# Two-layer backbone on one core: pooling mixer emitted one group later, products reordered, operand regions shifted, first and last classical tiles changed

## The chip, the cores and the metric

The program runs on one core of a Trainium2 chip. A core has a matrix engine (PE, whose weight loads the profile lists apart as PEld), a vector engine (DVE), a scalar engine (ACT), a general engine (POOL) and a queue processor (SP). Each works through its own instruction list in order and waits on semaphores for the others. The metric is the device time of one launch, in microseconds (us). Data is staged in on-chip SBUF; matmuls write PSUM.

## The reference, cut to what matters

```python
for i in range(2):                                   # layer 0: mLSTM mixer, layer 1: pooling mixer
    sh1, sc1, g1, sh2, sc2, g2 = split(silu(c) @ ada_w[i] + ada_b[i], 6)
    xn = rmsnorm(x, norm1_g[i]) * (1 + sc1) + sh1
    if i == 0:
        y = mlstm_mixer(xn, cn, ...)                 # projections, chunkwise scan in two directions, output product
    else:                                            # rows of 64 tokens, 4 groups of 256 channels
        p = centred_mean(xn, window of the group: 2, 4, 8 or 16) - xn
        y = einsum(p, pool_w[group]) * pool_scale
    x = x + g1 * y
    u = rmsnorm(x, norm2_g[i]) * (1 + sc2) + sh2
    x = x + g2 * (square(relu(u @ w1[i])) @ w2[i])   # 1024 -> 4096 -> 1024
return rmsnorm(x, final_g)                           # x: 1024 tokens x 1024 channels, float32
```

## The kernel before

All work is in float32. A big product is made of three matmuls on split operands (`mm3`, L169): weight-high by input-high, weight-high by input-low, weight-low by input-high. `split` (L165) makes the high part on ACT (L166) and the low part on DVE (`sub`, L163). The activations x lie feature-major in SBUF as tiles of [128, 2, 512]: four tiles for each of the two token halves (hf = 0 and 1).

A scheduler orders each engine's list: it simulates the program, and where several instructions are ready the code that was emitted first goes first. So the place of a `yield` in a generator, and the windows in which generators are woven together, decide the order.

One MLP goes in these stages.

1. `up_halves`: a few blocks of 128 hidden channels ("classical": 6 in layer 0, 12 in layer 1) are computed for one token half at a time by `up_half` (L858), eight k blocks of three matmuls into one PSUM bank. The inputs are uh (high, made by DVE L818 and ACT L819) and ul (low, DVE L820); the weights w1h and w1l come from ACT and DVE.
2. `flow`: the other hidden channels go through a scheme with seven products for eight, and their results hs are stored to DRAM on POOL's queue (L950).
3. Still in `flow`: 16 early classical steps of the second product (two for each of eight output blocks m; PSUM tile pd), then the passes: products (PSUM tile pe) whose operands hop are read back by `load_op` (L1005) on POOL's queue into two rings of buffers, A (12) and T (16), as the table RING says. A third ring B (4) holds raw hidden channels.
4. The classical tiles of the second product: first all output blocks of half 0, then those of half 1. Their operands hc are split from hr, which SP reads back. A step is one output block by one chunk of the hidden channels. The result goes into x by DVE (L1180).

`beside` runs side generators in windows of the main one's steps: `mods1` (layer 1's adaLN vectors: 48 loads of 256 KB on POOL's queue and a DVE product each, L237 and L238) in the window MO; the pooling mixer `pool(0)` and the norm of half 0 for layer 1's MLP in the windows ML, beside the classical tiles of layer 0; `pool(1)` and the norm of half 1 beside `up_halves(1, 0)` in the window MU.

A norm's statistics are: the squares of x (ACT L298) summed over the tiles into acc (L300, on DVE or POOL), a small matmul pc over partitions (L273), rv (DVE L275), a power on POOL (L276), dgr (DVE L279), a matmul rbp that spreads the result (L281), and a copy rbs (ACT L284). From rbs the next u is made (L818, L819, L820). `pool(hf)` makes for each of four groups a padded copy up (L1258), sums s over shifted copies (L1263, L1267), corrections at the row edges (POOL, L1275), the difference pt (L1276), and then, at once, the matmul pp (L1284) and the update of x (L1286).

Two places are called turns below: turn 1, from the end of layer 0's classical tiles to the first blocks of layer 1 (half 0), and turn 2, from half 0 to half 1 of those blocks.

In the address of a partition, tiles of ring A begin on a multiple of 256 bytes, those of T 96 bytes past one, those of B 128 bytes past one; weight tiles begin on one. The inputs uh and ul lie in A (for half 1, those of the first two tiles in B), their combinations th and tl, which the seven-product scheme takes, in T. Of the matmuls with 512 columns, 3,300 in the program read their moving operand from A, 504 from B and 2,904 from T.

Of the kernel before, what the change touches and what calls it, by code (L numbers as in the profile page):

```python
# [15 lines left out]
P = 128  # L16
D = 1024
T = 1024
# [44 lines left out]

MO = (49, 16, 86)
ML = ((12, 2, 12), (10, 12, 20))
MU = (34, 0, 10)
# [20 lines left out]
class Net:  # L87
    def __init__(self, ctx, tc, io, dbg=None):
        self.tc = tc
        self.nc = tc.nc  # L90
        self.io = io
        self.ctx = ctx
        e = ctx.enter_context
        self.psA = e(tc.tile_pool(name="psA", bufs=1, space=bass.MemoryType.PSUM))
        self.bank = 0
        self.alt = 0
        self.psN = e(tc.tile_pool(name="psN", bufs=2, space=bass.MemoryType.PSUM))
        self.psC = e(tc.tile_pool(name="psC", bufs=1, space=bass.MemoryType.PSUM))
        self.dr = e(tc.tile_pool(name="dr", bufs=1, space=bass.MemoryType.DRAM))
        self.sb = e(tc.tile_pool(name="sb", bufs=1))  # L100
        self.gx = ExitStack()
        self.gp = self.gx.enter_context(tc.tile_pool(name="gp", bufs=1))
        self.r = None
# [754 lines left out]
    def up_half(self, l, f, hf):  # L858

        nc = self.nc  # L860
        hi, lo = self.load_w(self.io["w1"][l, f], [P, KT, P], "w1")
        ps = self.pa([P, 512], "pu1")
        for k in range(KT):
            self.mm3(ps, hi[:, k], lo[:, k], self.uh[l][k // 2][hf][:, k % 2], self.ul[l][k // 2][hf][:, k % 2], k == 0, k == KT - 1)
        r = self.tmr([P, 512], "r")
        self.hidden(l, f, hf, r, ps)
# [138 lines left out]
    def load_op(self, l, i, q):  # L1005

        t = self.op16("hop", RING[(7 * i + q) % 28])
        self.nc.gpsimd.dma_start(out=t, in_=self.hs[l][i, q])  # L1008
        self.H[i, q] = t
# [9 lines left out]
    def flow(self, l):  # L1019
# [177 lines left out]
        for hf in range(2):  # L1197
            for m in order[:4] if l and hf else order:
                classical(hf, m, ch[hf][::-1] if hf == 0 and m == order[-1] else ch[hf], bank(new), 0, 512, True, result(hf, 0, 512))
        if l:  # L1200
            pn = [bank(lambda: self.pn("pd")) for _ in range(2)]
# [11 lines left out]
        steps[a:b] = self.turns(steps[a:a + 14], steps[a + 14:b])  # L1213
        ready, loads = [], 0
        for n, (_, _, run, what) in enumerate(steps):
            halves = n > b
# [11 lines left out]
            elif what == "C" and self.late:  # L1228
                self.late.pop(0)()
            pump()  # L1230
            yield


    def pool(self, hf):
# [7 lines left out]
        if hf:  # L1242
            yield from self.rstd(hf, g)
        rb = self.rb
        for a in range(4):
# [4 lines left out]
            pt = [tmp([P, 512], "pt") for _ in range(2)]  # L1250
            for i in range(2):
                k = 2 * a + i

                u = tmp([P, 8, 80], "up")
                g.memset(u[:, :, 0:8], 0.0)
# [3 lines left out]
                                       in1=rb.rearrange("p (r t) -> p r t", r=8), op0=ALU.mult, op1=ALU.mult)  # L1259
                nc.scalar.activation(t, t, AF.Identity, bias=self.mod[1][:, k:k + 1])  # L1260
                lo, hi = 1, 80
                s = tmp([P, 8, 80], "s")
                v.tensor_tensor(out=s[:, :, 1:80], in0=u[:, :, 0:79], in1=u[:, :, 1:80], op=ALU.add)  # L1263
                for b in range(a):
                    w = 1 << b
                    n = tmp([P, 8, 80], "s")
                    v.tensor_tensor(out=n[:, :, lo + w:hi - w], in0=s[:, :, lo:hi - 2 * w], in1=s[:, :, lo + 2 * w:hi], op=ALU.add)  # L1267
# [8 lines left out]
                v.scalar_tensor_tensor(out=pt[i].rearrange("p (r t) -> p r t", r=8), in0=s[:, :, 8:72], scalar=0.5 / w,  # L1276
                                       in1=u[:, :, 8:72], op0=ALU.mult, op1=ALU.subtract)
                yield
            pn = self.pn("pp")
            for i in range(2):  # L1280
                m = 2 * a + i
                ps = pn[:, i]
                for c in range(2):
                    nc.tensor.matmul(out=ps, lhsT=pw[:, c, P * i:P * i + P], rhs=pt[c], start=c == 0, stop=c == 1)  # L1284
                x = self.x[a][hf][:, i]
                v.scalar_tensor_tensor(out=x, in0=ps, scalar=self.pg[:, m:m + 1], in1=x, op0=ALU.mult, op1=ALU.add)  # L1286

            if a == 0:
                self.rs = self.rstd(hf)
            else:  # L1290
                next(self.rs)
            next(self.rs)
            yield

    def final(self, hf, lo, n, last=False):
# [100 lines left out]
    def run(self):  # L1396
        self.weng = None
        self.mark = None
        self.gate = None
        self.nw = 0  # L1400
        self.region("r1")
# [103 lines left out]
```

## Time and profile before

| | |
|---|---|
| median of 3 runs | 2058.02 us (2054.32 to 2061.98) |
| profiled execution, its own time | 2041.83 us |
| span, first to last instruction | 2039.7 us |
| mean granted PE clock, share of full | 0.981 |
| busy: PE / DVE / ACT / POOL | 1932.5 / 1387.6 / 868.7 / 415.2 us |
| chain that ended last, by engine | PE 65%, DMA 10%, DVE 10%, issue 9%, POOL 3%, ACT 2% |

Busy is the time in which an engine worked on an instruction; a wait is the idle time before an instruction, put down to what came last. A line of a kernel can be a helper's, so operations are told by their tiles (pd, pe, pu and ps are PSUM tiles of the products, ws and w1h/w1l weights). [...]

### The profile page before, as it was taken

How to read it: one execution, taken by the hardware profiler on the slowest of the kernel's cores; microseconds unless marked ns; L12 is line 12 of the kernel's file. 1: busy time of each engine (PE TensorE's matmuls, PEld its weight loads, DVE VectorE, ACT ScalarE, POOL GpSimd, SP SyncE). 2: the span in 40 equal slices, each digit the busy share in tenths (PEclk: the TensorE clock that was granted, in tenths of full speed). 3: DMA queues.
4: the chain of work that ended last, by engine and by line, in shares of the span. 5: the costliest groups of instructions: out<-in, count | busy, mean ns of one | idle time of the engine just before them, and what ended most of it. 6: DMA issues, size and time to landing. Idle time of an engine off the chain costs nothing.

```text
span 2039.7 us, 26798 instructions
## 1 busy us (share of the span) xinstructions
PE 1932.5 (95%) x9341; PEld 1544.0 (76%) x9341; DVE 1387.6 (68%) x2492; ACT 868.7 (43%) x1598; POOL 415.2 (20%) x595
## 2 busy tenths in 40 slices
PE   6999999988999999999999999798999998999998
PEld 3998877766777888887777777576888886886787
DVE  5587233878858688864777878587478855568644
ACT  4412222444436566654322233345557654222433
POOL 1222110454420011122332231210011120112010
PEclk9999999999999999999999999798999999999999
DMA  8499567665435366788888462154447696754642
GB/s 308 133 328 328 170 207 222 204 194 172 143 126 171 133 233 222 263 280 307 273 293 270 129 207 95 63 166 141 140 160 240 246 326 224 245 165 161 198 160 89
DMA packets 202167, 414.83 MB, mean 203 GB/s; under 512 B 18864, under 2 KB 108080, under 8 KB 202032
## 3 DMA queue, kind: packets, MB, share of 16 engines
q1 hardware_dynamic: 141936, 227.49, 35.1%
q0 software_dynamic: 43968, 157.31, 22.5%
q10 hardware_dynamic: 16128, 28.32, 3.7%
q8 instruction: 74, 1.21, 0.2%
q14 instruction: 61, 0.50, 0.1%
HBM read 303.31 MB, written 109.74 MB: 203 GB/s over the span
## 4 chain that ended last, share of the span: by engine, by line
PE 65%; DMA 10%; DVE 10%; issue 9%; POOL 3%; ACT 2%; SPq 1%; POOLq 0%; ACTq 0%; DVEq 0%
PE ps L172 22%; PE pd L172 11%; PE pu L172 9%; PE pb L172 6%; PE pe L172 6%; PE po L172 3%; DMA w<-in_w 2%; PE pv L172 1%; POOL adat L237 1%; DMA hr<-hd 1%; DMA qk<-kqd 1%; DMA xr<-xd 1%; PE pp L1284 1%; DVE ws L163 1%; PE pn L748 1%
## 5 line engine op out<-in xcount | busy, mean ns | idle before, releaser
L172 PE MATMUL pe<-hop,ws 128*128 128x512 f32 x1512 | 362.6, 398 | 12.5 <-DVE y L1097 6.2
L172 PEld LDWEIGHTS pe<-hop,ws 128*128 128x128 f32 x1512 | 283.3, 189 | 87.4 <-DVE y L1097 7.7
L172 PE MATMUL pd<-hc,ws 128*128 128x512 f32 (+1 forms) x1440 | 331.3, 386 | 10.4 <-ACT ws L166 4.3
L172 PEld LDWEIGHTS pd<-hc,ws 128*128 128x128 f32 x1440 | 257.5, 189 | 76.4 <-ACT ws L166 7.8
L166 ACT ACTIVATE ws<-w 128x384 fp32r<-128x384 f32 (+3 forms) x296 | 151.8, 529 | 335.8 <-PE pe L172 118.6
L163 DVE TENSOR_TENSOR ws<-w,ws 128x384 fp32r<-128x384 f32 (+3 forms) x296 | 176.0, 605 | 99.1 <-ACT ws L166 98.5
L172 PE MATMUL ps<-th,ws 128*128 128x512 f32 x736 | 242.5, 396 | 0.1
L172 PE MATMUL ps<-uh,ws 128*128 128x512 f32 x552 | 179.4, 391 | 0.0
L172 PEld LDWEIGHTS ps<-th,ws 128*128 128x128 f32 x736 | 138.4, 188 | 33.5 <-issue 0.5
L950 POOL DMA_DIRECT2D hs<-hs x126 | 67.2, 533 | 453.3 <-DVE hs L163 448.9
L172 PE MATMUL ps<-tl,ws 128*128 128x512 f32 x368 | 145.4, 395 | 0.0
L172 PE MATMUL pu<-ul,w1h 128*128 128x512 f32 x288 | 115.7, 402 | 11.2 <-DVE ul L820 11.2
L172 PE MATMUL pu<-uh,w1h 128*128 128x512 f32 x288 | 117.7, 410 | 5.5 <-ACT uh L819 4.6
L172 PEld LDWEIGHTS ps<-uh,ws 128*128 128x128 f32 x552 | 103.6, 188 | 23.4
L163 DVE TENSOR_TENSOR ws<-w1s,ws 128x512 fp32r<-128x512 f32 x138 | 94.7, 687 | 37.7 <-ACT ws L166 37.6
L172 PE MATMUL pu<-uh,w1l 128*128 128x512 f32 x288 | 116.6, 406 | 1.3 <-DVE w1l L163 1.3
L166 ACT ACTIVATE ws<-w1s 128x512 fp32r<-128x512 f32 x138 | 86.6, 629 | 71.7 <-PE ps L172 45.3
L1097 DVE TENSOR_TENSOR y<-pe,y 128x512 f32<-128x512 f32 x128 | 87.5, 686 | 43.1 <-PE pe L172 43.0
L1008 POOL DMA_DIRECT2D hop<-hs x126 | 66.8, 532 | 237.4 <-PE pe L172 143.9
L172 PE MATMUL ps<-ul,ws 128*128 128x512 f32 x276 | 108.1, 392 | 0.0
L935 DVE TENSOR_TENSOR o<-ps,o 128x512 f32<-128x512 f32 x115 | 79.1, 688 | 38.5 <-PE ps L172 35.9
L163 DVE TENSOR_TENSOR hs<-o,hs 128x512 fp32r<-128x512 f32 x126 | 85.8, 686 | 12.7 <-ACT hs L166 12.5
(288 smaller groups left out, 3785.8 us busy)
## 6 DMA issues: line engine op xcount, KB each, us to landing
hs<-hs POOLq DMA_DIRECT2D x126, 512.0 KB, 4.0
hop<-hs POOLq DMA_DIRECT2D x126, 512.0 KB, 5.7
w<-in_w SPq DMA_DIRECT2D x64, 512.0 KB, 4.0
adat<-in_adaT POOLq DMA_DIRECT2D x96, 256.0 KB, 4.8
w1s<-in_w SPq DMA_DIRECT2D x46, 512.0 KB, 5.1
w<-in_w SPq DMA_DIRECT2D x44, 384.0 KB, 3.6
ada<-in_adaT SPq DMA_DIRECT2D x32, 512.0 KB, 5.5
w<-in_w SPq DMA_DIRECT2D x60, 256.0 KB, 3.4
```

What stands on the lines that cost most here:

```text
L163: (eng or self.nc.vector).tensor_tensor(out=lo, in0=src, in1=hi.bitcast(F32), op=ALU.subtract)
L166: self.nc.scalar.activation(hi, src, AF.Copy)
L172: return self.nc.tensor.matmul(out=out, skip_group_check=more, **k)
L237: (nc.gpsimd if l else nc.sync).dma_start(out=w, in_=self.io["adaT"][48 * l + i - 16, :, n * q:n * q + n])
L748: nc.tensor.matmul(out=pn[:, a, d], lhsT=W[d][:, h], rhs=vs[:, h], start=False, stop=d == 1)
L935: self.mark = v.tensor_tensor(out=o[out], in0=o[p], in1=o[q], op=ALU.add)
L950: nc.gpsimd.dma_start(out=self.hs[l][i, q], in_=t)
L1008: self.nc.gpsimd.dma_start(out=t, in_=self.hs[l][i, q])
L1097: self.mark = v.tensor_tensor(out=y, in0=o[bank], in1=y, op=ALU.add)
L1284: nc.tensor.matmul(out=ps, lhsT=pw[:, c, P * i:P * i + P], rhs=pt[c], start=c == 0, stop=c == 1)
```

## The change

The parts of the diff are: other windows MO and ML; a tile of 160 bytes per partition allocated first, which moves the tiles behind it; the order of the 24 matmuls in `up_half`; a POOL copy of one element, that reads the sum evacuated by ACT for an output block, in every other early classical step, after which (and only then) operand loads are issued in these steps; the first two output blocks of half 1 taken in turns by chunk; and `pool`, in which the matmuls of a group come behind the preparation of the next, the edge corrections and half 1's sums acc move from POOL to DVE, pt is one tile and two buffers of s are used in turn.

```diff
-MO = (49, 16, 86)
-ML = ((12, 2, 12), (10, 12, 20))
+MO = (49, 34, 92)
+ML = ((14, 2, 9), (10, 9, 17))
...
+        self.sb.tile([P, 40], F32, name="pad", tag="pad", bufs=1)
...
     def up_half(self, l, f, hf):
...
-        for k in range(KT):
-            self.mm3(ps, hi[:, k], lo[:, k], self.uh[l][k // 2][hf][:, k % 2], self.ul[l][k // 2][hf][:, k % 2], k == 0, k == KT - 1)
+        us = [[u[l][k // 2][hf][:, k % 2] for k in range(KT)] for u in (self.uh, self.ul)]
+        for j, (w, u) in enumerate(((hi, us[0]), (lo, us[0]), (hi, us[1]))):
+            for k in range(KT):
+                self.nc.tensor.matmul(out=ps, lhsT=w[:, k], rhs=u[k], start=j + k == 0, stop=j == 2 and k == KT - 1)
...
     def load_op(self, l, i, q):
...
-        self.nc.gpsimd.dma_start(out=t, in_=self.hs[l][i, q])
+        d = self.nc.gpsimd.dma_start(out=t, in_=self.hs[l][i, q])
+        if self.pace is not None:
+            self.after(d, self.pace)
...
+            if hf:
+                n = 2 * len(ch[1])
+                steps[at:at + 2 * n] = [s for c in range(0, n, 2) for s in steps[at + c:at + c + 2] + steps[at + n + c:at + n + c + 2]]
...
+        n0 = self.pieces(l)[0]
...
-            pump()
+            if n0 <= n < n0 + 16:
+                if (n - n0) % 2:
+                    m = (n - n0) // 2
+                    self.pace = nc.gpsimd.tensor_copy(out=pace, in_=Y[m // 2][0][0:1, m % 2, 0:1])
+                    pump()
+                    self.pace = None
+            else:
+                pump()
...
     def pool(self, hf):
...
-            yield from self.rstd(hf, g)
+            yield from self.rstd(hf)
+        def mix(a, pw, pt):
+            pn = self.pn("pp")
...
-                        g.tensor_tensor(out=e, in0=e, in1=f, op=ALU.mult)
+                        v.tensor_tensor(out=e, in0=e, in1=f, op=ALU.mult)
...
+            if before:
+                mix(*before)
+            before = a, pw, pt
             yield
+        mix(*before)
+        yield
```

With the added tile, A tiles begin 160 bytes past a multiple of 256, B tiles 32 bytes past one, T tiles on one; weight tiles begin 160 bytes past one.

PE's order at turn 1 before: the last matmuls of the pooling mixer (pp), the classical tiles (pd), the statistics (pc, then rbp), and the first two blocks of layer 1 (pu, uh and ul, by w1h and w1l).

```order
L1284 MATMUL pp<-pt,pw 128x512 x2
L172 MATMUL pd<-hc,ws 128x512 x12
L273 MATMUL pc<-cst,acc 128x2 x4
L281 MATMUL rbp<-dgr,cst 128x512
L172 MATMUL pu_11376<-uh,w1h 128x512
L172 MATMUL pu_11425<-uh,w1h 128x512
L172 MATMUL pu_11376<-ul,w1h 128x512
L172 MATMUL pu_11376<-uh,w1l 128x512
L172 MATMUL pu_11376<-uh,w1h 128x512
```

The same place of the changed program:

```order
L1274 MATMUL pp<-pt,pw 128x512 x2
L174 MATMUL pd<-hc,ws 128x512 x30
L275 MATMUL pc<-cst,acc 128x2 x4
L174 MATMUL pd<-hc,ws 128x512 x3
L283 MATMUL rbp<-dgr,cst 128x512
L868 MATMUL pu_11369<-uh,w1h 128x512
L868 MATMUL pu_11418<-uh,w1h 128x512
L868 MATMUL pu_11369<-uh,w1h 128x512
L868 MATMUL pu_11418<-uh,w1h 128x512
```

30 classical matmuls instead of 12 stand between the mixer's last product and the statistics, three stand between pc and rbp where none stood, and 15 products with uh go in a row before the first w1l (and ul after those), where the third product was one with ul.

DVE's order at turn 1 before: from the mixer's update of x (y<-pp) to the first products with rbs. The names are those of the norm above.

```order
L163 TENSOR_TENSOR w1l<-w_11370,w1h 128x1024
L1286 SCALAR_TENSOR_TENSOR y<-pp,pg,y 128x512
L300 TENSOR_TENSOR acc<-acc,sq 128x512
L1180 SCALAR_TENSOR_TENSOR y<-pd,mod_95,y 128x512
L275 TENSOR_SCALAR rv<-pc 128x4
L163 TENSOR_TENSOR w1l<-w_11419,w1h 128x1024
L279 TENSOR_TENSOR dgr<-cst,rv 128x512
L818 SCALAR_TENSOR_TENSOR y<-y,gsc_98,rbs 128x512 x8
L820 SCALAR_TENSOR_TENSOR ul<-y,mod_96,uh 128x512 x8
```

DVE's order there in the changed program:

```order
L302 TENSOR_TENSOR acc<-acc,sq 128x512
L165 TENSOR_TENSOR w1l<-w_11363,w1h 128x1024
L277 TENSOR_SCALAR rv<-pc 128x4
L1186 SCALAR_TENSOR_TENSOR y<-pd,mod_96,y 128x512
L281 TENSOR_TENSOR dgr<-cst,rv 128x512
L302 TENSOR_TENSOR acc<-acc,sq 128x512 x2
L165 TENSOR_TENSOR w1l<-w_11412,w1h 128x1024
L302 TENSOR_TENSOR acc<-acc,sq 128x512
L820 SCALAR_TENSOR_TENSOR y<-y,gsc_99,rbs 128x512 x8
L302 TENSOR_TENSOR acc<-acc,sq 128x512
L822 SCALAR_TENSOR_TENSOR ul<-y,mod_97,uh 128x512 x7
```

The weight part w1l stands behind dgr instead of ahead of it, and half 1's sums acc, which POOL had, stand between DVE's other work.

POOL's order in the changed program, from the stores hs on, where before 28 loads hop and then 13 loads adat followed the stores in a row (dsh is the copied element):

```order
L954 DMA hs_5471<-hs 128x1024 x70
L1012 DMA hop<-hs_5471 128x1024 x11
L1247 COPY dsh<-y 1x1
L1012 DMA hop<-hs_5471 128x1024 x5
L1247 COPY dsh<-y 1x1
L1012 DMA hop<-hs_5471 128x1024
L1247 COPY dsh<-y 1x1
L1012 DMA hop<-hs_5471 128x1024
```

Eleven loads go at once, five behind the first copy, and then mostly one behind each; the loads adat begin behind all of them, two at a time between later loads hop.

## Rows read from the trace of the kernel before

**Rows 1.** The page: busy time, share and instructions of each engine.

```profile
PE 1932.5 (95%) x9341; PEld 1544.0 (76%) x9341; DVE 1387.6 (68%) x2492; ACT 868.7 (43%) x1598; POOL 415.2 (20%) x595
```

**Rows 2.** Waits of PE at turn 1: us in total, times, longest.

```profile
PE pu L172 <- DVE ul L820: 7.3, 1, 7.3
PE rbp L281 <- DVE dgr L279: 5.1, 1, 5.1
PE pu L172 <- ACT uh L819: 2.3, 1, 2.3
```

**Rows 3.** Waits of PE at turn 2.

```profile
PE pu L172 <- DVE ul L820: 3.9, 1, 3.9
PE pu L172 <- ACT uh L819: 2.2, 1, 2.2
PE rbp L281 <- DVE dgr L279: 1.6, 1, 1.6
```

**Rows 4.** Waits of PE at the start of layer 0's passes, 945 to 985 us.

```profile
PE pe L172 <- DVE y L1097: 1.8, 1, 1.8
PE pe L172 <- DVE ws L163: 1.0, 1, 1.0
PE pe L172 <- ACT y L1095: 0.9, 2, 0.7
PE pe L172 <- ACT ws L166: 0.5, 1, 0.5
```

**Rows 5.** Wait of PE where half 1's classical tiles begin, 1170 to 1225 us.

```profile
PE pd L172 <- ACT hc L166: 3.6, 1, 3.6
```

**Rows 6.** Waits of PE at layer 1's early classical steps, 1660 to 1720 us.

```profile
PE pd L172 <- ACT ws L166: 3.0, 3, 1.0
PE pe L172 <- ACT ws L166: 1.8, 1, 1.8
PE pe L172 <- DVE ws L163: 0.9, 1, 0.9
```

**Rows 7.** Timeline of turn 1: start, us, engine, instructions, what ended the idle time.

```profile
1290.30 3.36 PE L172 MATMUL pd<-hc,ws 128*128 128x512 f32 x12
...
1295.28 1.01 POOL L276 TENSOR_TENSOR rv<-rv,nhalf 128x4 f32<-128x4 f32 x1 [17.46 <-DVE rv L275]
...
1297.04 1.22 DVE L163 TENSOR_TENSOR w1l<-w,w1h 128x1024 fp32r<-128x1024 f32 x1 [1.85 <-ACT w1h L166]
...
1298.19 1.75 DVE L279 TENSOR_TENSOR dgr<-cst,rv 128x512 f32<-128x512 f32 x1
...
1303.47 8.79 DVE L818 SCALAR_TENSOR_TENSOR y<-y,gsc,rbs 128x512 f32<-128x512 f32 x7
...
1312.18 4.05 DVE L820 SCALAR_TENSOR_TENSOR ul<-y,mod,uh 128x512 fp32r<-128x512 f32 x6
```

**Rows 8.** Windows: width, busy PE, PEld, DVE, ACT, POOL, PEclk, DMA share, GB/s.

```profile
930.00:950.00 20.00, 20.00 (x90) 16.57 (x89) 5.49 (x13) 8.86 (x21) 2.11 (x4) 1.00 1.05 371
1680.00:1700.00 20.00, 16.00 (x65) 11.26 (x64) 4.85 (x14) 6.03 (x16) 4.14 (x8) 1.00 1.12 391
1304.00:1314.00 10.00, 2.25 (x5) 1.34 (x6) 10.00 (x10) 6.32 (x10) 5.27 (x4) 0.50 0.00 0
1324.00:1394.00 70.00, 70.00 (x279) 52.01 (x278) 49.27 (x62) 32.98 (x49) 5.35 (x28) 1.00 0.49 157
```

**Rows 9.** Groups of instructions by line and form: busy, mean ns of one.

```profile
L300 POOL TENSOR_TENSOR acc<-acc,sq 128x512 f32<-128x512 f32 x28 | 41.4, 1479 | 81.0 <-ACT sq L298 77.9 <-issue 2.7
L300 DVE TENSOR_TENSOR acc<-acc,sq 128x512 f32<-128x512 f32 x35 | 24.2, 692 | 8.5 <-ACT sq L298 7.1
L1275 POOL TENSOR_TENSOR s<-s,inv 128x8 f32<-128x8 f32 x8 | 3.5, 433 | 28.1 <-DVE s L1263 28.1
L172 PE MATMUL ps<-th,ws 128*128 128x512 f32 x736 | 242.5, 396 | 0.1
L172 PE MATMUL ps<-uh,ws 128*128 128x512 f32 x552 | 179.4, 391 | 0.0
```

More of the change, by code (lines that the diff above doesn't have):

```diff
@@ L1197, in flow @@
         for hf in range(2):
-            for m in order[:4] if l and hf else order:
+            ms = order[:4] if l and hf else order
+            at = len(steps)
+            for m in ms:
                 classical(hf, m, ch[hf][::-1] if hf == 0 and m == order[-1] else ch[hf], bank(new), 0, 512, True, result(hf, 0, 512))
+            if hf:
+                n = 2 * len(ch[1])
+                steps[at:at + 2 * n] = [s for c in range(0, n, 2) for s in steps[at + c:at + c + 2] + steps[at + n + c:at + n + c + 2]]
         if l:
@@ L1214, in flow @@
         ready, loads = [], 0
+        n0 = self.pieces(l)[0]
+        pace = self.small([P, 4], "dsh", 1)[0:1, 0:1]
         for n, (_, _, run, what) in enumerate(steps):
@@ L1242, in pool @@
         if hf:
-            yield from self.rstd(hf, g)
+            yield from self.rstd(hf)
         rb = self.rb
+        def mix(a, pw, pt):
+            pn = self.pn("pp")
+            for i in range(2):
+                m = 2 * a + i
+                ps = pn[:, i]
+                for c in range(2):
+                    nc.tensor.matmul(out=ps, lhsT=pw[:, c, P * i:P * i + P], rhs=pt[:, c], start=c == 0, stop=c == 1)
+                x = self.x[a][hf][:, i]
+                v.scalar_tensor_tensor(out=x, in0=ps, scalar=self.pg[:, m:m + 1], in1=x, op0=ALU.mult, op1=ALU.add)
+            if a == 0:
+                self.rs = self.rstd(hf)
+            else:
+                next(self.rs)
+            next(self.rs)
+        before = None
         for a in range(4):
@@ L1249, in pool @@
             nc.sync.dma_start(out=pw, in_=self.io["poolw"][a].rearrange("c p d -> p c d"))
-            pt = [tmp([P, 512], "pt") for _ in range(2)]
+            pt = self.op16("pt", "T" if hf else "A", F32)
+            us = [tmp([P, 8, 80], "up") for _ in range(2)]
+            ss = [tmp([P, 8, 80], "s") for _ in range(2 if a else 1)]
             for i in range(2):
                 k = 2 * a + i
-                u = tmp([P, 8, 80], "up")
+                u = us[i]
                 g.memset(u[:, :, 0:8], 0.0)
@@ L1260, in pool @@
                 nc.scalar.activation(t, t, AF.Identity, bias=self.mod[1][:, k:k + 1])
+            for i in range(2):
+                u = us[i]
                 lo, hi = 1, 80
-                s = tmp([P, 8, 80], "s")
+                s = ss[0]
                 v.tensor_tensor(out=s[:, :, 1:80], in0=u[:, :, 0:79], in1=u[:, :, 1:80], op=ALU.add)
@@ L1265, in pool @@
                     w = 1 << b
-                    n = tmp([P, 8, 80], "s")
+                    n = ss[(b + 1) % 2]
                     v.tensor_tensor(out=n[:, :, lo + w:hi - w], in0=s[:, :, lo:hi - 2 * w], in1=s[:, :, lo + 2 * w:hi], op=ALU.add)
@@ L1274, in pool @@
                         f = inv[:, r].unsqueeze(1).to_broadcast([P, 8, r.stop - r.start])
-                        g.tensor_tensor(out=e, in0=e, in1=f, op=ALU.mult)
-                v.scalar_tensor_tensor(out=pt[i].rearrange("p (r t) -> p r t", r=8), in0=s[:, :, 8:72], scalar=0.5 / w,
+                        v.tensor_tensor(out=e, in0=e, in1=f, op=ALU.mult)
+                v.scalar_tensor_tensor(out=pt[:, i].rearrange("p (r t) -> p r t", r=8), in0=s[:, :, 8:72], scalar=0.5 / w,
                                        in1=u[:, :, 8:72], op0=ALU.mult, op1=ALU.subtract)
                 yield
[L1279 to L1292, printed above, removed]
+            if before:
+                mix(*before)
+            before = a, pw, pt
             yield
+        mix(*before)
+        yield
     def final(self, hf, lo, n, last=False):
@@ L1399, in run @@
         self.gate = None
+        self.pace = None
         self.nw = 0
```

## The prediction

> **What bounds the kernel now.** I read the page's first part, then PE's waits stretch by stretch, then the timeline of the stretch with the longest waits, and last the windows around it. PE is busy for 1932.5 of 2039.7 us [rows 1], so a change pays in two ways alone: by closing a gap on PE, or by changing what one product costs. The other engines are far from full (DVE 68%) and matter where PE waits for them.
>
> The gaps that the change touches are few. At turn 1 PE waits 7.3 us for ul, 5.1 for dgr and 2.3 for uh, 14.7 in all [rows 2]. At turn 2 it waits 3.9, 2.2 and 1.6, in all 7.7 [rows 3]. At the start of layer 0's passes it loses 1.8 + 1.0 + 0.9 + 0.5 = 4.2 [rows 4], at the start of half 1's classical tiles 3.6 for one operand hc [rows 5], and in layer 1's early classical steps 3.0 + 1.8 + 0.9 = 5.7 for split weights [rows 6]. Together that is 35.9 us, 1.8% of the span, and an upper limit of what reordering can give, but for the clock: after the gaps of turn 1 PE stands at half its clock, .50 from 1304 to 1314 us [rows 8], so the first products behind a gap take longer as well.
>
> **Turn 1.** Two causes show in the timeline [rows 7]. First, the chain pc, rv, power, dgr, rbp has nothing on PE beside it, and in it a weight part w1l of 1.22 us goes on DVE ahead of dgr, which then takes 1.75 us while a POOL sum runs beside it. Second, the third product of the first block needs ul, and DVE makes all eight L818 before the first L820: those L818 take 8.79 us for seven, 1.26 each, with POOL busy 5.27 of 10 us beside them [rows 8], whereas the L820 behind them take 4.05 for six, 0.68 each.
>
> The change acts on both. The order has w1l behind dgr, three classical matmuls between pc and rbp, 15 products with uh in a row, and the sums off POOL. What is left, worked out:
> - From pc to rbp. The power takes 1.0 us [rows 7]; I put dgr at 0.7, the time of a DVE operation of that size (a sum takes 0.692 [rows 9]), and add some 0.7 for rv and the hand-overs. That is 2.4. Three matmuls cover three times 3.36 / 12 = 0.28, say 0.8. Left: 1.6 of 5.1.
> - From rbp to the first uh: copy, one L818, one ACT operation, with nothing beside it. It stays at 2.3.
> - The products with uh. Eight L818 at 0.68 give 5.4 us in which PE can do two blocks' 16 products at about 0.23 (the length of a product at full clock: twelve take 3.36 us [rows 7], some of it the last one's run-out) = 3.7. Left: 1.7. Then come 16 products with w1l, 3.7 us. The eight L820 want 5.4 us, but they have begun when the last L818 ends; with three sums of 0.69 put between them DVE ends some 7.5 us after that, and PE's 16 products with w1l and 16 with ul (7.4 us) need the last ul only at the end. Left: about 0.
>
> The sum is 5.6 of 14.7: a gain of 9. Its bounds are 0 (DVE, which takes on 7 sums of 0.692 here, is late with everything) and the whole 14.7. With the gaps the stretch at half clock shrinks; behind 1313 us PE still runs some 4 us at the low level, at twice the time per product. I take 1 us of gain, bounds 0 and 2.
>
> **Turn 2.** The same order of products takes away the wait of 3.9 for ul, but PE then runs into the pace of L818 as above, 1.7 left. Six products instead of two stand between pc and rbp: 4 times 0.23 = 0.9 less. The wait for uh stays. Left 4.8 of 7.7: a gain of 3. Bounds: 7.7, and a loss of 5, if the mixer of half 1 ends late. For the sums now on DVE (7 times 0.692 = 4.8 us) and 28 edge corrections come on top of DVE's work before turn 2. DVE has 49.3 of 70 us busy there [rows 8]; a correction took 0.433 us on POOL in its smallest form [rows 9]; DVE has no row for that form, so I price it between 0.1 and 0.45 us, take 0.3, and for the 14 of one half get 4 us. That fits into the 20 us that are free: cost 0. If the cover is gone it is up to 5 us, which is the bound taken.
>
> **The mixer a group later.** For half 0 the last pp now has 30 classical matmuls behind it instead of 12, about 7 us that hide its update of x, its sum and pc. It adds no instruction to PE. Cost 0, within turn 1's bounds.
>
> **mods1 from step 34 instead of 16.** The adaLN loads (256 KB each) leave the stretch in which the passes start, where the DMA engines are full (1.05 of their time, 371 GB/s, at 930 to 950 us [rows 8]). I expect 3 of the 4.2 us of waits [rows 4] to go. But the 48 DVE products and the loads are then squeezed into 58 steps instead of 70, beside the same ring of operand loads on POOL's queue; I set 1.5 against it. Gain 1.5; bounds 4.2 and a loss of 3.
>
> **Operand loads paced.** In layer 1's early steps 28 loads of 512 KB compete with the weights at a share of 1.12 [rows 8], and PE waits for weights that ACT splits late [rows 6]. Spread out, 2.5 of 5.7 us go. The copy makes the loads behind it on POOL wait for ACT's evacuation of an output block; what is queued behind are operand loads alone, 16 of which have been let go by the second copy. A late one would hold a pass: a loss of up to 3. Bounds 5.7 and -3.
>
> **First two output blocks of half 1 in turns.** Each chunk's hc is needed one step, of 9 to 12 products, later: at 0.28 us each about 3. Of 3.6 [rows 5], 3 go; bounds 3.6 and 0.
>
> **The shifted addresses.** The products with th and tl lie in ring T and take 396 ns, those with uh in ring A 391, with the same weights in the same stage [rows 9]: 5 ns for an operand 96 bytes past a multiple of 256 against one on it, if it is the address that makes it. The change puts T on a multiple and A, B and the weights off one. What 160 or 32 bytes past cost, and what a weight tile pays, no row shows. If only T changes: 2,904 products by 4.5 ns = 13 us gain. If T gains and A and B pay as T did: 3,804 by 4.5 = 17 loss, net 4 loss. If the weights pay too: 30 more. I take 0, near the middle of the first two.
>
> [...] The rows differ by the 5 ns above, without saying that the address is why.
>
> **The sum.** 9 + 1 + 3 + 1.5 + 2.5 + 3 = 20 us less than the profiled execution's 2041.83 gives 2021.8. The median of the runs shown lies at 2058.02, 0.8% above that execution, so the forecast for it is 2058.02 x 2021.8 / 2041.83 = 2037.8: 1.0% faster. The layer 0 mLSTM, the first 30% of the span, keeps its order and pays at most the shift.
>
> **The rivals.**
> - A: DVE becomes what PE waits for at the turns. The sums and corrections leave POOL, which is 20% busy, for DVE, and they stand in DVE's list among w1l and u. For it: DVE is full (10.00 of 10 us) exactly where PE waits [rows 8]. Against: a sum takes 692 ns there and 1479 on POOL [rows 9], and DVE's slow L818 ran beside POOL. Of the 12 us at the turns nothing is gained: profiled 2034, median about 2050.
> - B: the address is the reason for the 5 ns, and A at 160 and B at 32 pay nothing: 13 us on top of the forecast, 2008.8, median 2025. For it: two groups of 736 and 552 products differ. Against: A and T may differ for another reason, and A's new place is no multiple either.
> - C, on the slower side: weight tiles off a multiple pay as moving operands do, at every product, and A and B pay too. T's moving gain (13) is then met by its weights' loss (13), and A and B lose twice 17: +34, less 20, is +14: profiled 2056, median 2072. It makes the kernel slower than before from 20 / 6,708 = 3 ns net for each 512-column product. For it: the rows for T. Against: weight loads overlap the products (PEld is busy 1544 us beside PE's 1932 [rows 1]), so there is slack for them.
>
> **How the numbers follow.** A measurement of this kernel can tell about 0.5%, 10 us, from no change: faster is below 2047.7, slower above 2068.3. Forecast 0.58, A 0.19, B 0.13, C 0.10. The forecast's own terms scatter from about 2028 to 2050, so I give it 0.52 faster, 0.06 the same. A is the same in 0.15, and 0.02 on either side. B is faster. C is slower in 0.09 and the same in 0.01. That makes 0.67 faster, 0.22 the same, 0.11 slower. The range reaches from 2022, below B, to 2063, between A and C, and leaves out most of C and the tails; the likeliest case's own range is 2028 to 2050.
>
> **What would show it.** At turn 1 of the changed kernel PE's waits for ul are gone, that for dgr is near 1.6 us, L818 take 0.7 each, and the clock is below full for less time. At turn 2 no wait for ul stands, and no wait behind the mixer's last pc is longer than before. The three short waits of rows 4 to 6 are smaller. The mean product with th falls to 391 ns if the address counts, and that with uh rises to 395 if A pays; other weights' products (pv, the scan's) would rise as well if C holds. I am wrong if PE's busy time outside the turns moves by more than 10 us, or if a new wait for DVE of over 5 us stands before either turn.

## The result, and the profile after

The changed kernel took 2033.47 us (median of four runs, 2030.07 to 2038.10) against 2056.17 for the kernel before in the same comparison: a ratio of 0.989, 95% interval 0.985 to 0.992. Forecast were 2037.8 us and 1.0% faster.

The two profiled executions differ by less: 2038.1 and 2041.83 us. They start with 600 us of instructions in the same order, and these took 613.1 us in the changed kernel and 606.7 in the kernel before. The first profile of before was also one of that kernel's quickest executions: two later profiles, of before and of before with the shift alone, took 2051.35 and 2050.40. So the stretches are compared one by one, between the times at which PE starts the first product of each stage in the trace. Before is the mean of these three profiles, after the mean of two (the changed kernel, and the changed kernel without the shift):

| stretch | before, us | after, us | difference |
|---|---|---|---|
| up to layer 0's half blocks (nothing reordered) | 607.0 | 615.3 | +8.3 |
| layer 0's half blocks | 70.3 | 67.9 | -2.4 |
| seven products, early classical steps | 276.1 | 276.3 | +0.2 |
| passes and classical tiles, to layer 1's first product | 356.6 | 358.5 | +1.9 |
| half blocks of half 0, from turn 1's first product to turn 2's rbp | 94.6 | 86.1 | -8.5 |
| turn 2's rbp and half blocks of half 1 | 77.4 | 73.2 | -4.3 |
| seven products of layer 1 | 192.0 | 192.1 | 0.0 |
| its early classical steps | 28.1 | 24.9 | -3.2 |
| its passes | 145.1 | 143.5 | -1.6 |
| its classical tiles and the end | 198.4 | 197.6 | -0.9 |

Behind the first row the sum is -18.8 us. The first row scatters from 605 to 618 us between profiles of kernels that have the same instructions there, and the fourth from 352 to 360 among the three profiles of before alone, so small differences in these two say nothing.

Two rows hold a little of their neighbours. The row of half 0 ends behind PE's wait for turn 2's dgr, which fell by 1.0 us. And before, the first two products of layer 1's passes stand ahead of the last four classical ones: the row of its early steps holds 104 products before and 108 after, so that, at 0.23 us for each (half 0's products start 0.227 us apart at full clock, before, from 1393.73 to 1395.32 us), like for like this row gained 4.1 and the passes 0.7.

PE's waits at turn 1, changed kernel (us in total, times, longest), the answer to [rows 2]:

```profile
PE pu L868 <- ACT uh L821: 3.9, 1, 3.9
PE pc L275 <- POOL acc L302: 3.6, 1, 3.6
PE rbp L283 <- DVE dgr L281: 2.8, 1, 2.8
```

The wait for ul is gone and that for dgr has halved; that for uh has grown by 1.6. The second line is not of turn 1: it is the mixer's first statistics, at 1232 us, some 80 us earlier. At turn 2, against [rows 3]:

```profile
PE pu L868 <- ACT uh L821: 2.6, 1, 2.6
PE pu L868 <- ACT w1h L168: 1.4, 1, 1.4
PE rbp L283 <- DVE dgr L281: 0.6, 1, 0.6
```

Waits at the passes' start (945 to 985 us), at their end (1115 to 1170) and in layer 1's early steps and the passes' start behind them (1660 to 1720), against [rows 4] and [rows 6]:

```profile
PE pe L174 <- DVE y L1103: 2.3, 1, 2.3
...
PE pd L174 <- ACT ws L168: 3.2, 1, 3.2
PE pe L174 <- DVE pw L1103: 1.9, 1, 1.9
PE pe L174 <- DVE y L1103: 1.6, 2, 1.3
...
PE pe L174 <- ACT pw L1101: 0.7, 1, 0.7
PE pe L174 <- ACT y L1101: 0.7, 1, 0.7
PE pe L174 <- DVE ws L165: 0.6, 1, 0.6
```

The first fell from 4.2 to 2.3 and the last from 5.7 to 2.0. The middle one, 6.7, stood at 3.0 before. From 985 to 1115 us, between the first two, waits rose from 0.5 (1.1 and 1.3 in the other profiles of before) to 1.9. Windows of the changed kernel (columns as in [rows 8], PEclk the granted clock as a share of full) show where the time at the passes' end went, and what the clock does at turn 1:

```profile
1130.00:1150.00 20.00, 14.57 (x61) 10.86 (x60) 19.97 (x37) 5.08 (x9) 8.29 (x13) 0.97 0.59 198
1150.00:1160.00 10.00, 10.00 (x32) 7.92 (x33) 7.59 (x21) 2.61 (x5) 1.79 (x1) 0.71 0.19 66
1304.00:1314.00 10.00, 7.23 (x34) 5.63 (x33) 3.57 (x7) 2.73 (x4) 1.01 (x1) 0.94 0.45 142
1314.00:1324.00 10.00, 6.11 (x15) 3.80 (x14) 8.68 (x13) 9.12 (x15) 0.00 (x0) 0.55 0.32 110
```

At the passes' end DVE has no free time, 19.97 of 20 us: eight of the 48 products of mods1 fall there (6 us), against two in the same 20 us with the old window. PE waits, and in the next 10 us its mean granted clock is .71. DVE is not all of it. The longest wait, 3.2 us, is for weights that ACT splits as soon as their load lands:

```profile
1149.21 0.63 ACT L168 ACTIVATE ws<-w 128x512 fp32r<-128x512 f32 x1 [2.11 <-DMA w<-in_w]
```

DVE's split of an hc let this load go at 1144.4 us, and its two parts took 3.7 and 4.3 us to land, beside six adaLN loads in the same 20 us; with the old window such a pair took 2.2 and 3.2. So 3.5 of the 6.7 us are waits for DVE itself, and of the other 3.2 about 1 is the slower transfer.

At turn 1 PE is at .55 of its clock in one window of 10 us and near full (.94) ahead of it. The kernel before was at .50 in one window [rows 8] and well below full in both beside it:

```profile
1294.00:1304.00 10.00, 3.04 (x10) 1.41 (x10) 4.81 (x6) 5.08 (x9) 5.70 (x5) 0.66 0.53 189
...
1314.00:1324.00 10.00, 10.00 (x42) 8.36 (x41) 4.56 (x9) 1.24 (x2) 1.02 (x1) 0.82 0.00 0
```

The timeline of turn 1, changed kernel, against [rows 7]:

```profile
1301.41 7.56 PE L174 MATMUL pd<-hc,ws 128*128 128x512 f32 x30
...
1309.62 0.95 PE L174 MATMUL pd<-hc,ws 128*128 128x512 f32 x3
...
1310.08 1.23 DVE L165 TENSOR_TENSOR w1l<-w,w1h 128x1024 fp32r<-128x1024 f32 x1 [5.86 <-ACT w1h L168]
1311.22 0.16 DVE L277 TENSOR_SCALAR rv<-pc 128x4 f32<-128x4 f32 x1
...
1312.50 0.69 DVE L281 TENSOR_TENSOR dgr<-cst,rv 128x512 f32<-128x512 f32 x1 [0.47 <-POOL rv L278]
...
1313.34 2.05 PE L283 MATMUL rbp<-dgr,cst 128*128 128x512 f32 x2 [2.77 <-DVE dgr L281]
1314.82 1.06 ACT L168 ACTIVATE w1h<-w 128x1024 fp32r<-128x1024 f32 x1 [1.55 <-DMA w<-in_w]
1315.79 0.61 ACT L300 ACTIVATE sq<-y 128x512 f32<-128x512 f32 x1
...
1316.31 0.58 ACT L286 ACTIVATE rbs<-rbp 128x512 f32<-128x512 f32 x1
...
1317.06 0.68 DVE L302 TENSOR_TENSOR acc<-acc,sq 128x512 f32<-128x512 f32 x1
1317.66 4.72 DVE L820 SCALAR_TENSOR_TENSOR y<-y,gsc,rbs 128x512 f32<-128x512 f32 x7
...
1319.27 3.36 PE L868 MATMUL pu<-uh,w1h 128*128 128x512 f32 x7 [3.89 <-ACT uh L821]
```

The weight part that stood ahead of dgr now stands behind it, but that of the block before stands ahead of rv: DVE does it from 1310.08 us on, and rv starts 1.1 us later. dgr takes 0.69 us for 1.75, and DVE's products with rbs 0.67 each for 1.26. But when rbp ends, at 1315.39, ACT is on a weight part and then on half 1's square sq, so rbs starts 0.9 us late; and DVE, which has a weight part and one sum of half 1 to do, starts its first product with rbs 0.8 us behind rbs. These two make the 1.6 us by which the wait for uh grew.

The groups of products that were to tell of the address, against [rows 9]:

```profile
L174 PE MATMUL ps<-th,ws 128*128 128x512 f32 x736 | 242.6, 396 | 0.8 <-DVE o L939 0.8
L174 PE MATMUL ps<-uh,ws 128*128 128x512 f32 x552 | 179.4, 392 | 0.2 <-ACT o L959 0.2
```

Nothing moved, though T now begins on a multiple of 256 bytes and A 160 past one.

### The profile page after: what moved, and what is told of

The parts are those of the page before. It is cut to its first block, busy times and chain, and to the rows that moved or that the text cites. A ratio compares the mean times of both kernels' runs of the same rounds, so it can differ in the third digit from the quotient of the medians.

```text
span 2036.2 us, 26763 instructions
## 1 busy us (share of the span) xinstructions
PE 1934.8 (95%) x9341; PEld 1547.5 (76%) x9341; DVE 1383.4 (68%) x2527; ACT 866.1 (43%) x1598; POOL 398.6 (20%) x576
## 4 chain that ended last, share of the span: by engine, by line
PE 68%; DMA 11%; DVE 8%; issue 7%; POOL 3%; ACT 2%; SPq 1%; POOLq 0%; ACTq 0%; DVEq 0%
PE ps L174 21%; PE pd L174 12%; PE pu L868 10%; PE pe L174 8%; PE pb L174 6%; PE pv L174 3%; PE po L174 3%; DMA w<-in_w 2%; DMA qk<-kqd 2%; DMA hr<-hd 1%; PE pp L1274 1%; POOL hop L1012 1%; POOL adat L239 1%; DMA ada<-in_adaT 1%; DVE ws L165 1%
## 5 line engine op out<-in xcount | busy, mean ns | idle before, releaser
L168 ACT ACTIVATE ws<-w 128x512 fp32r<-128x512 f32 (+3 forms) x296 | 152.5, 529 | 346.7 <-PE pe L174 143.6
L165 DVE TENSOR_TENSOR ws<-w,ws 128x512 fp32r<-128x512 f32 (+3 forms) x296 | 175.5, 604 | 94.0 <-ACT ws L168 93.6
L165 DVE TENSOR_TENSOR hs<-o,hs 128x512 fp32r<-128x512 f32 x126 | 85.8, 686 | 13.1 <-ACT hs L168 13.0
L168 ACT ACTIVATE hs<-o 128x512 fp32r<-128x512 f32 x126 | 77.1, 623 | 28.4 <-DVE o L951 17.9
L239 POOL DMA_DIRECT2D adat<-in_adaT x96 | 52.1, 543 | 171.2 <-DVE adat L240 119.1
L868 PE MATMUL pu<-uh,w1h 128*128 128x512 f32 x288 | 76.0, 408 | 8.5 <-ACT uh L821 6.5
```

What stands on the lines that cost most here:

```text
L165: (eng or self.nc.vector).tensor_tensor(out=lo, in0=src, in1=hi.bitcast(F32), op=ALU.subtract)
L168: self.nc.scalar.activation(hi, src, AF.Copy)
L239: (nc.gpsimd if l else nc.sync).dma_start(out=w, in_=self.io["adaT"][48 * l + i - 16, :, n * q:n * q + n])
L868: self.nc.tensor.matmul(out=ps, lhsT=w[:, k], rhs=u[k], start=j + k == 0, stop=j == 2 and k == KT - 1)
```

## The experiments

All ratios are to the kernel before. Stretches are those of the table above, each from the one profile of its run.

**The kernel before once more, and the shift by itself.**

> The kernel before, unchanged, to see how far its executions scatter and where. Its profiled execution took 2041.83 us while its four timed runs took 2053 to 2062; the changed kernel's profiled execution took 2038.1 and its timed runs 2030 to 2038. Theory 1 (the gain is closed gaps of PE, about 20 us, and the profiled execution of before was a quick one by chance): ratio 1.00, a new profile near 2053 to 2060, longer than the first one in the layer 0 mLSTM or in its gaps, not in the time of a product. Theory 2 (the timed runs of before are slower than profiled ones for a reason that the profile takes away): the new profile is again near 2042 and the timed runs near 2056.

> Before, with the 160-byte tile alone. Theory 1 (the address does nothing, since the products from T take as long after the shift as before it, 396 ns, and those from A 391 to 392): ratio 1.000 within 0.4%. Theory 2 (the shift gives what the closed gaps of the profile, some 10 us behind 620 us, do not explain of the 22.7): ratio 0.993 to 0.995. Theory 3 (the shift costs, A, B and weights off a multiple of 256): ratio above 1.003.

> The changed kernel without the 160-byte tile. Theory 1 (address worth nothing): ratio to before 0.989, as with it. Theory 2 (the shift gives about 12 us): 0.994 to 0.996. Theory 3 (it costs): under 0.986.

The second is before with this line alone, the third the changed kernel without it:

```diff
+        self.sb.tile([P, 40], F32, name="pad", tag="pad", bufs=1)
```

Measured: before again 1.0004 (0.9988 to 1.0021), profiled execution 2051.35; the shift alone 1.0003 (0.9989 to 1.0017); the changed kernel without it 0.9905 (0.9887 to 0.9922), against 0.9888 (0.9853 to 0.9922) with it. The address is worth nothing that these runs can tell, with the rest of the change or without it. The first profile's 2041.83 was a quick execution: the new one is 7.4 us longer from layer 0's half blocks on, mostly in the stretch of the passes and classical tiles.

**The order of products in the half blocks.** First the order alone in the kernel before, then the changed kernel with the old order. The edit is the part of the diff in `up_half`, done and undone.

> Before, with the new order of the 24 products in the half blocks alone. Theory 1 (PE waits for ul at the turns and the order takes these waits away): the waits for ul of 7.3 and 3.9 us go, 4 to 8 us come off in all, ratio 0.996 to 0.998. Rival (DVE's pace binds and the wait moves to uh and dgr): ratio 1.000, the waits at turn 1 still 13 us or more in sum.

> The changed kernel with the old order of products in the half blocks. Theory 1 (turn 1 needs both: the sums off POOL make the L818 quick, 0.68 us for 1.18, and the order keeps ul out of the way; turn 2 and layer 0's blocks take their gain from the order alone): stretch of layer 0's half blocks 70.3 us again for 67.9, turn 2 and behind 77.4 for 73.2, a wait for ul at turn 1 of 4 to 5 us (7.3 in the kernel before), in sum 10 to 12 us lost, ratio 0.994 to 0.996. Rival (the moved engines carry turn 1 by themselves): turn 1's stretch stays at 86 us, ratio 0.992.

Measured: order alone 0.9974 (0.9958 to 0.9989). Layer 0's half blocks took 67.9 us and turn 2's stretch 73.3, both as in the changed kernel; turn 1's stretch took 94.9, as before. PE's waits around turn 1 in that kernel (1110 to 1340 us):

```profile
PE rbp L281 <- DVE dgr L279: 5.1, 1, 5.1
...
PE pu L866 <- ACT uh L819: 4.1, 5, 2.3
```

No wait for ul is left, and PE waits five times for uh instead, at the pace of DVE's slow products with rbs. The waits are 9.2 us for 14.7, and yet no time is gained there. The clock shows why. The windows are the whole stretch, first the kernel before, then the order alone:

```profile
1304.46:1399.15 94.69, 85.82 (x339) 64.37 (x340) 64.87 (x82) 42.25 (x62) 12.18 (x34) 0.93 0.38 123
1311.70:1406.56 94.86, 90.33 (x339) 66.54 (x340) 64.98 (x82) 41.28 (x62) 12.12 (x34) 0.91 0.36 126
```

The same 339 products keep PE busy 4.5 us longer. PE comes out of the chain of pc and rbp at the lower clock (.50 in the first 10 us of both). Before, it then waited, with two products done; with the new order it works, at 0.43 us a product for 0.23. Until the clock rose, 13 us after the first product before and 16 here, 11 products had run at the lower clock before, and 26 here.

With the old order in the changed kernel the ratio was 0.9965 (0.9950 to 0.9979); the three stretches took 70.3, 91.6 and 77.0 us, 11.7 more than the changed kernel's, and the waits around turn 1 (1185 to 1345 us) were:

```profile
PE pc L275 <- POOL acc L302: 4.3, 1, 4.3
PE pu L174 <- DVE ul L822: 3.9, 1, 3.9
PE pu L174 <- ACT uh L821: 3.9, 1, 3.9
PE rbp L283 <- DVE dgr L281: 2.2, 1, 2.2
```

The wait for ul is 3.9 instead of 7.3: half of it goes without the order, with the new mixer, whose sums are off POOL (DVE's products with rbs take 0.68 us each there, 1.18 with the order alone). Turn 1 needs both parts. Turn 2 and layer 0 need the order alone. Both rivals fall, the first one's in the total and in the sum of the waits; but turn 1's time did not fall with the order alone, and the clock is the reason.

**The mixer.** The changed kernel with `pool` and ML of before.

> The changed kernel with the mixer and its windows ML of before (matmuls at once, sums and edge corrections on POOL). Theory 1 (turn 1's gain goes with the sums off POOL, since the order of products alone left that stretch at 94.9 us, as before): the stretch from the first product of layer 1 is 94 to 95 us, L818 take 1.1 us or more, PE waits about 5 us for dgr, ratio 0.994 to 0.996. Rival (mixer a group later and engines moved are worth nothing once the order is changed; the gain of 8 us at that stretch comes from another part, the turns of the first two blocks): the stretch stays near 86, ratio 0.990.

Measured: 0.9958 (0.9939 to 0.9976). Turn 1's stretch took 92.5 us, 6.4 more than the changed kernel's; PE waits 5.3 us for dgr and five times for uh, 4.1 in all. These are the waits of the order alone, whose stretch took 94.9 us, and 94 to 95 were expected here. Only the clock differs: it was back at full 10 us after the first product instead of 16. So of the 8.5 us of that stretch the order alone gives 0, all but the mixer 2, all but the order 3, and both the whole. Which part of the mixer does it, the sums moved to DVE or the matmuls a group later, these runs do not separate.

**The first two output blocks in turns.** The changed kernel without this:

```diff
-            if hf:
-                n = 2 * len(ch[1])
-                steps[at:at + 2 * n] = [s for c in range(0, n, 2) for s in steps[at + c:at + c + 2] + steps[at + n + c:at + n + c + 2]]
```

> The changed kernel without the first two output blocks of half 1 taken in turns. Theory 1 (the 3.6 us for hc went, and pc of the mixer's first statistics now waits 3.6 us for POOL's last sum at the same place, so nothing was gained): hc is waited for 3 to 4.4 us again, pc for 0 to 1, sum of both the same within 1.5 us, ratio 0.989 to 0.991. Rival (the prediction's term): 3 us slower, and pc's wait stands beside the one for hc.

Measured: 0.9926 (0.9895 to 0.9958). Its waits from 1185 to 1345 us:

```profile
...
PE pd L174 <- ACT hc L168: 3.3, 1, 3.3
PE rbp L283 <- DVE dgr L281: 2.9, 1, 2.9
```

hc is waited for 3.3 us, and pc not at all. With the turns it is pc, 3.6, and hc not at all. One wait stands in the place of the other. The times do not decide it: the stretch took 358.6 us, and 361.3 and 355.7 in the two profiles with the turns, and the ratio's interval reaches from the changed kernel to 0.6% above. But the trace of the changed kernel shows that both are waits for one load:

```profile
1225.19 0.74 DVE L1186 SCALAR_TENSOR_TENSOR y<-pd,mod,y 128x512 f32<-128x512 f32 x1
1228.99 1.06 ACT L168 ACTIVATE hc<-hr 128x1024 fp32r<-128x1024 f32 x1 [4.97 <-DMA hr<-hd]
1229.95 0.61 ACT L300 ACTIVATE sq<-y 128x512 f32<-128x512 f32 x1
1230.71 1.72 POOL L302 TENSOR_TENSOR acc<-acc,sq 128x512 f32<-128x512 f32 x1 [5.98 <-ACT sq L300]
1232.48 1.87 PE L275 MATMUL pc<-cst,acc 128*128 128x2 f32 x8 [3.63 <-POOL acc L302]
```

The last y of half 0 is ready at 1225.9 us. Its square stands behind an hc in ACT's list, ACT waits 5 us for the load of that hc, and so the square comes 4 us late, and POOL's sum and pc with it. PE no longer waits for hc itself, but for a sum that hangs on the same load.

**mods1's window.** The changed kernel with MO of before.

> The changed kernel with mods1's window of before, (49, 16, 86). Theory 1 (the later window costs more than it gives: at the passes' end, 1130 to 1150 us, DVE is busy 19.97 of 20 us with the products moved there, and PE waits 1.3 + 1.9 + 0.3 for DVE and 3.2 for weights split late, with the clock at .71 behind it, against 1.9 us of waits saved at the passes' start): the waits at 1115 to 1170 us fall from 6.7 to about 3, those at 945 to 985 rise from 2.3 to 4.2, DVE at the passes' end is below full, and the time falls by 2 to 5 us, ratio 0.987 to 0.988 against before (the changed kernel had 0.9888, without the shift 0.9905). Rival (the window is worth the 1.5 us of the prediction's term): ratio 0.990 to 0.991, waits at the end unchanged.

Measured: 0.9925 (0.9900 to 0.9950), not faster: the number was missed. From 985 to 1185 us PE's waits fell from 10.4 to 4.3 us, as theory 1 had it, but at the passes' start they rose from 2.3 to 6.1 (one of 4.2 for ACT's weights), pc waited 4.8 us for 3.6 and dgr 4.1 for 2.8 (uh at turn 1 2.9 for 3.9). The stretch of passes and classical tiles took 358.2 us, within the 355.7 to 361.3 of the later window. These runs show no gain of either window on the other.

**The pacing of the operand loads.** The changed kernel without the copies, loads let go as before.

> The changed kernel without the copies that pace the operand loads in the early classical steps. Theory 1 (the paced loads leave the DMA engines to the weights; that is the 3 us that the stretch of layer 1's early steps lost, 27.9 to 28.6 us before, 24.5 to 25.0 in all variants with pacing): the stretch takes 27.5 to 28.6 us again with waits of 3 us or more for ACT's split weights, ratio 0.991 to 0.992. Rival (the address or the order of the half blocks in front made that stretch shorter): it stays under 25.5.

Measured: 0.9951 (0.9931 to 0.9970). The stretch of layer 1's early steps took 28.0 us, 3.0 to 3.5 more than in every kernel with pacing, which have the same 108 products there. The waits from 1640 to 1730 us:

```profile
PE pe L174 <- DVE ws L165: 2.8, 1, 2.8
PE pd L174 <- ACT ws L168: 2.4, 3, 1.0
```

That is the place and size of theory 1. But the ratio is worse than the changed kernel's by 0.5%, some 10 us, and these 3.3 us explain a third of it. The profiled execution (2036.0) was the quickest of that kernel's runs (2036 to 2048), so the rest can't be looked up in it. Layer 0's early steps are paced as well; without it PE waits 0.7 us for 2.3 at the passes' start and 5.2 for 1.9 from 985 to 1115 us, but up to 1185 us 10.5 in all for 12.7, so no loss shows there. The changed kernel itself was timed in the first comparison alone, so the two ratios come from different ones. The rest stays open.

**A mended kernel.** Three edits in the changed kernel, and two of them by themselves:

```diff
-MO = (49, 34, 92)
+MO = (49, 25, 89)
...
-ML = ((14, 2, 9), (10, 9, 17))
+ML = ((14, 6, 12), (10, 12, 18))
...
-... (self.rstd(0, nc.gpsimd, order=self.order(0)), 8, n[2] + 3, n[3] + 3), ...
+... (self.rstd(0, order=self.order(0), hold=True), 8, n[2] + 3, n[3] + 7), ...
```

The first is mods1's window, the second the engine of the first statistics' sums (DVE, without nc.gpsimd), the third hold, with the later windows ML and n[3] + 7; hold makes the pc matmuls depend on the product emitted last. The kernel with two edits has neither hold nor the later windows: there MO and the engine of the sums alone differ from the changed kernel.

> The changed kernel with three mendings: mods1's window halfway, (49, 25, 89); the sums of the mixer's first statistics on DVE instead of POOL; their pc held back behind the sixth step of half 1 and the mixer's windows moved to ((14, 6, 12), (10, 12, 18)). Theory 1 (three new waits ate the gain: 3.6 us of pc for POOL's sum, about 5 us at the passes' end for a full DVE): pc's wait is under 1 us, the waits at 1115 to 1170 us fall to 3, the later mixer gives 0.7 us back at turn 1; 4 to 6 us faster than the changed kernel, ratio 0.986 to 0.988 against before. Rival (these waits only move on to the next step, as the one for hc did): same as the changed kernel, 0.990 to 0.991, with waits of like size on the mixer's pp or at turn 1.

> The changed kernel with two of these mendings: mods1's window (49, 25, 89) and the first statistics' sums on DVE; pc not held back. Theory 1: pc's wait falls by the difference of one sum, 1.7 to 0.7 us, to about 2.6, the waits at the passes' end fall as in the kernel with three mendings, turn 1 stays; 2 to 4 us faster than the changed kernel, ratio 0.987 to 0.989. Rival: no difference, 0.990 to 0.991.

Measured: three edits 0.9855 (0.9831 to 0.9880), median 2023.72 us; two edits 0.9860 (0.9835 to 0.9884), median 2026.86. These are the fastest kernels of the study, by ratio 0.3 to 0.5% below the changed one; their intervals lie below that of the changed kernel without the shift, and overlap the wider one of the changed kernel itself. The windows of the first at the passes' end:

```profile
1130.00:1150.00 20.00, 19.25 (x83) 15.27 (x82) 18.07 (x32) 5.66 (x10) 6.99 (x9) 1.00 0.35 119
1150.00:1160.00 10.00, 10.00 (x45) 8.08 (x44) 9.37 (x20) 1.44 (x5) 2.31 (x2) 1.00 0.35 105
```

DVE has some room again, PE is busy 19.25 of 20 us for 14.57, and the clock stays at full. (The passes of this kernel start 7 us earlier, so the windows are not the same work; but in no 10 us from 1100 to 1170 us is DVE busy for more than 9.64.) The stretch of passes and classical tiles took 352.9 and 351.6 us for the changed kernel's 355.7 and 361.3. Holding pc back took its wait away (2.9 with two edits, where its square still stands behind the split of that hc; none with three), but dgr at turn 1 was then waited for 4.8 us instead of 2.2, since the mixer ends later: it moved on, and the two kernels can't be told apart. What gained is the window halfway together with the sums on DVE; the runs do not separate these two.

## Why the prediction was right, point by point

**What bounds it: right.** PE is as busy as before (1934.8 us for 1932.5, and 1933.3 and 1936.7 in the other two profiles), the products of the seven-product scheme took as long, and the gain is closed gaps and less time at the lower clock, most of it at the places named.

**Turn 1: the size nearly right, its parts not.** Forecast: 9 us and 1 for the clock. The stretch lost 8.5, of which 1.0 is turn 2's dgr; ahead of it the wait for dgr lost 2.3, and that for uh grew by 1.6. That makes 8.2. The clock's 1 us is right: PE is busy 84.8 us in the stretch for 85.8, at a mean granted clock of .98 for .93. Of the 14.7 us of waits [rows 2] 6.7 are left, where the prediction had 5.6 with 1.7 of trickle among them. dgr was put at 1.6 and is 2.8: the order showed one w1l moved behind dgr, and I did not see that the w1l of the block before stands ahead of rv, where it takes 1.23 us of the same chain. Without it the wait would be, by an estimate from these two numbers, about the 1.6 of the forecast. uh was said to stay at 2.3 and is 3.9: I had counted half 1's sums into DVE's later work, and not the square and the weight part that ACT does between rbp and rbs, nor what DVE does ahead of its first product with rbs. The trickle of uh, put at 1.7, did not come. That both parts are needed, as the prediction had it ("the change acts on both"), the order alone and the change without the order showed: 0 and 3 of 8.5 us. What the order alone costs at the lower clock, 4.5 us, the prediction had not seen.

**Turn 2: the mechanism right, the gain larger.** Forecast 3; measured 4.3 in the stretch and 1.0 for dgr ahead of it. The waits left are 4.6 us, where the forecast had 4.8 (its own terms, 1.7, 2.2 and 0.7, add up to 4.6). They are others than forecast: the trickle of 1.7 did not come, but 1.4 for a weight part w1h did, which stood at 0.5 before. That the two sums agree is chance. The rest of the gain, 1.6 us, is the clock, for which the prediction had a term at turn 1 alone: PE is busy 69.2 us in the stretch for 70.8, with the same products, at a mean granted clock of .98 for .91. The bound of a loss through DVE was not needed: the edge corrections took 0.17 to 0.22 us each on DVE, below the 0.3 that I put in.

**Layer 0's half blocks: a term left out.** The sum has no term for this stretch; it lost 2.4 us, by the order of products alone. Its waits for weights before (w1l 1.3 us, w1h 0.5) go with the same order that brings w1l eight products later.

**The mods window: wrong.** Forecast a gain of 1.5. The start gained 1.9 of the 3 put, but at the end of the window, which I priced at 1.5, waits rose by 3.7, and PE's clock fell behind them (.71 from 1150 to 1160 us). The step that failed is "squeezed into 58 steps instead of 70 ... I set 1.5 against it": the price was of the queue of loads, and what bound was mostly DVE's time from 1130 to 1150 us (19.97 of 20 us busy), with about 1 us for a slower load. Undone, it gave nothing either, since the start then paid. The kernels with the window halfway were faster than both ends, but they had the sums on DVE as well.

**Pacing: right in the stretch.** Forecast 2.5, measured 4.1 like for like, and 3.0 to 3.5 with the pacing undone. That the whole kernel lost some 10 us without it is not explained.

**Blocks in turns: wrong.** Forecast 3; in the waits nothing is gained, 3.6 for pc in place of 3.3 for hc. "Each chunk's hc is needed one step, of 9 to 12 products, later" is true, and the wait for hc went. What the prediction did not ask is what else hangs on that hc's load: pc, which stands next in PE's order, needs a square that ACT does only behind its split of the same hc.

**The address: right.** Forecast 0; the products' means stayed at 396 and 391 to 392 ns, the shift alone gave 0 within 0.2%, and the changed kernel without it lay 0.2% from the one with it, inside both intervals. Rivals B and C fall with it. The 5 ns between T's products and A's are real and have another reason, which was not looked for.

**Rival A: wrong at the turns, for which it was made.** They gave 13.5 us of 13. DVE did become what PE waits for, but at the passes' end, through mods1's window.

So the total of 20 us came out (18.8 by stretches, 22.7 by the medians), but not from the terms that were summed. Turn 1 gave 8.2 us for 10, turn 2 5.3 for 3, and the pacing 4.1 for 2.5. Blocks in turns and mods, 4.5 us of the sum, gave nothing that these runs show: without turn 1's 0.7 us, the row that holds them is 2.6 us longer, which is within its scatter. Layer 0's half blocks gave 2.4 that were not in the sum, and layer 1's passes and last tiles 1.6 that no experiment here accounts for. That the errors nearly cancel is luck.

## What to carry to other kernels

A wait that goes at one place is gained only if the next instruction in that engine's order is ready (here 3.6 us for pc stood in the place of 3.3 for hc): look at what stands behind the waiting one, and whether it hangs, through another engine's order, on the same load, before writing down the whole wait. Where two causes hold up the same stretch (a late operand, and a slow producer), taking away one alone may gain nothing (0 of turn 1's 8.5 us with the order alone), so try parts together and alone; and where the clock is low behind a gap (.50 at turn 1), work that is moved there runs slowly (0.43 us a product for 0.23), so count busy time as well as waits. And when work is moved into a narrower window, price it by the busiest engine's free time in that window.

## What the runs showed of the hardware

The seven-product scheme's products with th, in ring T, take 396 ns and those with uh, in ring A, 391 to 392, in every kernel here, whether T begins on a multiple of 256 bytes and A 160 past one, or T 96 past one and A on one. A DVE operation of 512 columns that took 0.67 to 0.69 us by itself took 1.26 on the mean with POOL's sums (1479 ns on the mean) beside it. Single operations of the changed kernel also took longer beside one of POOL:

```profile
1140.30 1.50 POOL L1134 TENSOR_TENSOR y<-y,rbs 128x512 f32<-128x512 f32 x1
1140.57 1.64 DVE L165 TENSOR_TENSOR ws<-s,ws 128x384 fp32r<-128x384 f32 x1
...
1146.96 1.63 POOL L1134 TENSOR_TENSOR y<-y,rbs 128x512 f32<-128x512 f32 x1 [3.91 <-DVE y L1103]
1147.40 1.48 DVE L890 TENSOR_TENSOR s<-w 128x256 f32<-128x256 f32 x1
```

DVE's two took 0.55 and 0.42 us in other places; here they took 1.64 and 1.48, and each ends 0.3 to 0.4 us behind POOL's operation. Why they take longer there is not shown. There were three such operations in the 20 us in which DVE had no free time (the third took 1.65 us for 0.55), together some 3 us longer than in other places.

A stretch at the lower clock cost little while PE waited in it and much while PE worked in it: with the order alone the same 339 products took PE 90.3 us instead of 85.8.

A kernel of 2050 us had executions from 2044 to 2063 us with the same instructions, and the first 600 us, the same in every kernel here, scattered by 12 us between profiles, so that effects of 3 us are read from stretches and not from the total.
